# mLSTM mixer: turned rows one unit later, the gates' columns behind four tiles of values, the keys' last casts pinned

## The chip, the cores and the metric

The kernel runs on one core of a Trainium2 chip. The metric is the time of one execution in microseconds on the device, the median of several runs. TensorE (PE in the profile) does the matmuls and transposes, VectorE (DVE) and ScalarE (ACT) the elementwise work, GpSimd (POOL) some of it, and SyncE (SP) issues the transfers.

## What is computed

A network of two layers over 256 latent and 256 context tokens of width 1024: each layer is a half feed-forward, a mixer, and another half feed-forward, each with a residual norm. The first mixer is attention, the second the mLSTM that the change touches. Cut to that mixer:

```python
def mlstm_mixer(xl, xc, w_in, gate_b, conv_w, conv_b, norm_g, w_out):
    # p = xs @ w_in for both streams, split in q,k | v | o | g
    # q, k = silu(centred_conv(qk)); four heads, q and k of 128, v of 256
    # g: input and forget gates, forward and backward
    ...
    # forward and backward scans over the context, then over the latents
    o_lat = readout(hl_f + flip(hl_b), ol)

def readout(h, o):
    mu = jnp.mean(h, axis=-1, keepdims=True)
    var = jnp.mean(jnp.square(h - mu), axis=-1, keepdims=True)
    hn = (h - mu) * lax.rsqrt(var + LN_EPS)
    hn = hn.transpose(...).reshape(B, L, D_MODEL) * norm_g
    return (hn * jax.nn.sigmoid(o)) @ w_out
```

Per head and direction the scan is a masked, weighted product: with gate sums as exponents, `s = (q k^T) * exp(...)`, `num = s v`, `h = num / max(|sum of s|, exp(-m))`.

## The kernel before

**Tiling.** Activations stand transposed in `self.h`, eight tiles of 128 features by 512 tokens (latents in columns 0 to 255, context behind). Every float32 operand of a matmul is split into a high part (a cast to fp32r on ACT) and a low part (the rest, a subtraction on DVE), in `split` (lines 202 to 209). A product is then three matmuls, `mm3` (lines 221, 224, 225) or, with tokens as rows, `token_product` (lines 770 to 772): high by high, high by low, low by high. Weights are streamed in chunks of 128 by 1024: `raw` (line 189) loads one through SP's queue into one of three buffers, `chunk` splits it into one of seven buffers. `Keep` holds the chunks it has seen.

**What sets the order.** The program is written in the order of its data, and a scheduler of the framework lays out each engine's queue from it, by its own estimate of when operands are ready; each engine then runs its queue strictly in that order. `self.pin` ties an instruction behind the instruction that was written just before it on the same engine, and nothing else. So an instruction written later can still be queued earlier, unless it is pinned to one that is not.

**The mixer** (`mlstm`, from line 995). In order: queries, gates and keys are projected (`product`), latents first, while the norm of the context (`self.steps`, `norm`) is still being finished on ACT (line 496) and DVE (lines 495, 497); then the context half of the gates and keys. `gate_rows` (lines 1195 to 1235) turns the gates into rows of 64 by 512 on DVE and ACT; its `columns` (line 1237 on) transposes them (line 1240), and a copy (line 1242) leaves `kd` and `em`, the columns that later exponentials take as bias. Values follow: two blocks of four token tiles, 24 matmuls of 128 by 512 each; their casts are at line 1069, their low parts at line 1074. `residual` (lines 518 and 519) finishes the residual stream of an earlier norm, two tiles at a time.

**Units.** Eight units follow, head by head and in both directions: `inner` makes a head's scores (line 1082), the exponents in PSUM (lines 1092 and 1094), the weights by exponentials on ACT (lines 1099, 1112) and multiplications on DVE (lines 1102, 1114), their high parts (line 1104 on ACT, and `split`) and low parts (line 1105 on POOL, and `split`). `outer` of the unit before multiplies them by the values (lines 1127 to 1129), divides (lines 1131 to 1137), and, when both directions are summed, normalises the head's rows: statistics (1143, 1144), an inverse root of small DVE steps (233 to 247, 1146), and the scaling on ACT (line 1148). In the same step stand the products of the output gate (`OAT`, tanh at line 1171, line 1172 on POOL). `gated` transposes the head's normalised rows (line 1154, four transposes) and multiplies them by the gate on DVE (line 1157). Behind the units all eight tiles are split and multiplied by `w_out`: three output tiles first over inputs 0 to 5, then over inputs 6 and 7.

## Time and profile before

| | us |
|---|---|
| median of 3 runs | 1683.31 |
| lowest, highest | 1680.69, 1686.05 |
| the profiled execution | 1685.48 |
| its span, first to last instruction | 1683.7 |

The profiled execution's mean granted TensorE clock is 0.996. The mLSTM mixer takes about 1320 to 1483 us of the span. TensorE's busy time in parts of it (the windows of the trace):

| stretch, us | length | PE busy | granted clock |
|---|---|---|---|
| 1322 to 1364: queries, gates, keys, first values | 42 | 39.36 | 1.00 |
| 1364 to 1370: values, with the gates' columns | 6 | 6.00 | 1.00 |
| 1370 to 1400: values | 30 | 30.00 | 1.00 |
| 1400 to 1408: end of values, first unit | 8 | 7.50 | 1.00 |
| 1408 to 1470: units and the start of the out projection | 62 | 58.69 | 0.97 |

How to read it: a timeline row is start, duration, engine, line, operation and its tiles; in brackets stand the idle time of the engine ahead of it and what ended it. Matmuls overlap, so that the distance of their starts, not their duration, is the rate. A wait list row is who waited for whom, total, number, longest. A granted clock below 1.00 means that matmuls run slower by that factor.

### The profile page before, as it was taken

The numbers are of one execution on the slowest core, as the hardware profiler recorded it, in microseconds if no ns is written. First come the engines' busy times: TensorE is split into PE (matmuls) and PEld (weight loads), VectorE is DVE, ScalarE is ACT, GpSimd is POOL, SyncE is SP. The second block draws the span as 40 slices with busy tenths as digits, with TensorE's granted clock in tenths as the row PEclk, the third lists the DMA queues.
The fourth block names the chain that finished last, engine by engine and source line by source line (L and its number), as shares of the span: only waits on it lengthen the run. The fifth ranks groups of instructions, "written<-read, shape, count | busy, mean of one in ns | idle before, by whom it ended". The sixth has DMA issues, their size and how long they took to land.

```text
span 1683.7 us, 24582 instructions
## 1 busy us (share of the span) xinstructions
PE 1647.9 (98%) x9492; PEld 1441.9 (86%) x9492; DVE 1209.9 (72%) x2458; ACT 668.5 (40%) x1116; POOL 72.8 (4%) x82
## 2 busy tenths in 40 slices
PE   9999999999989999999999999999999999999998
PEld 6888888899977998888888998888889978999987
DVE  5899977659798889995334877643335866898687
ACT  5532123215665352222221443222222655656542
POOL 0000000001010100000000100000000101120000
PEclk9999999999999999999999999999999999999999
DMA  9577755412103247674222357642221332337552
GB/s 365 190 230 232 250 200 190 149 63 90 43 1 118 96 138 236 230 242 142 100 90 74 101 178 246 214 150 100 95 93 65 103 128 76 113 126 240 178 183 88
DMA packets 71909, 250.36 MB, mean 149 GB/s; under 512 B 7920, under 2 KB 10736, under 8 KB 71792
## 3 DMA queue, kind: packets, MB, share of 16 engines
q1 hardware_dynamic: 71216, 248.00, 43.5%
q8 instruction: 74, 1.21, 0.3%
q10 hardware_dynamic: 576, 0.79, 0.1%
q14 instruction: 43, 0.35, 0.1%
HBM read 247.71 MB, written 1.05 MB: 148 GB/s over the span
## 4 chain that ended last, share of the span: by engine, by line
PE 83%; DVE 10%; ACT 3%; issue 2%; DMA 1%; DVEq 0%; ACTq 0%; SPq 0%
PE t L221 23%; PE t L224 23%; PE t L225 23%; PE t L1255 4%; PE t L698 4%; DVE t L209 3%; ACT t L204 1%; PE t L771 1%; PE t L772 1%; PE t L770 1%; PE t L402 1%; DVE t L497 1%; DVE t L495 1%; DVE t L422 0%; DMA t<-in_ffn_in 0%
## 5 line engine op out<-in xcount | busy, mean ns | idle before, releaser
L221 PE MATMUL t<-t,t 128*128 128x512 f32 (+2 forms) x2532 | 852.8, 339 | 8.4 <-ACT t L204 5.8
L224 PE MATMUL t<-t,t 128*128 128x512 f32 (+2 forms) x2532 | 856.3, 339 | 1.2 <-DVE t L497 0.3
L225 PE MATMUL t<-t,t 128*128 128x512 f32 (+2 forms) x2532 | 853.1, 338 | 1.2 <-DVE t L209 1.1
L209 DVE TENSOR_TENSOR t<-t,t 128x256 fp32r<-128x256 f32 (+3 forms) x669 | 463.0, 726 | 203.8 <-ACT t L204 202.7
L204 ACT CAST t<-t 128x1024 fp32r<-128x1024 f32 (+3 forms) x453 | 377.1, 857 | 561.9 <-PE t L225 302.8
L221 PEld LDWEIGHTS t<-t,t 128*128 128x128 f32 x2532 | 475.9, 189 | 62.9 <-ACT t L204 8.0
L224 PEld LDWEIGHTS t<-t,t 128*128 128x128 f32 x2532 | 477.6, 189 | 55.8 <-DVE t L209 1.2
L225 PEld LDWEIGHTS t<-t,t 128*128 128x128 f32 x2532 | 477.2, 189 | 54.5 <-DVE t L209 2.1
L312 DVE SCALAR_TENSOR_TENSOR t<-t,t 128x1024 bf16<-128x1024 f32 x224 | 262.6, 1220 | 14.6 <-DMA t<-in_ada_w 14.0
L544 DVE TENSOR_TENSOR t<-t,t 128x512 f32<-128x512 f32 (+1 forms) x93 | 54.0, 585 | 116.1 <-PE t L225 95.7
L543 ACT ACTIVATE t<-t 128x512 f32<-128x512 f32 (+1 forms) x93 | 47.5, 514 | 196.7 <-PE t L225 196.6
L771 PE MATMUL t<-t,t 128*128 128x256 f32 (+1 forms) x256 | 79.3, 310 | 1.4 <-DVE t L209 1.4
L579 DVE SCALAR_TENSOR_TENSOR t<-t,t,t 128x256 f32<-128x256 f32 x96 | 42.7, 478 | 52.0 <-PE t L225 52.0
L770 PE MATMUL t<-t,t 128*128 128x256 f32 (+1 forms) x256 | 79.4, 310 | 0.0
L772 PE MATMUL t<-t,t 128*128 128x256 f32 (+1 forms) x256 | 78.9, 309 | 0.0
L439 POOL TENSOR_TENSOR t<-t,t 128x256 f32<-128x256 f32 x30 | 24.3, 809 | 1159.2 <-ACT t L429 1157.8
L1255 PE MATMUL t<-t,t 128*128 128x512 f32 (+3 forms) x286 | 60.8, 368 | 1.7 <-ACT t L1332 1.0
L698 PE MATMUL t<-t,t 128*128 128x512 f32 (+1 forms) x300 | 60.5, 364 | 0.0
L1255 PEld LDWEIGHTS t<-t,t 128*128 128x128 f32 (+2 forms) x286 | 43.8, 159 | 18.9 <-issue 3.6
L698 PEld LDWEIGHTS t<-t,t 128*128 128x128 f32 x300 | 51.5, 189 | 8.9
L429 ACT ACTIVATE t<-t 128x256 f32<-128x256 f32 x72 | 26.2, 412 | 66.9 <-DVE t L422 66.9
L771 PEld LDWEIGHTS t<-t,t 128*128 128x128 f32 x256 | 48.2, 188 | 4.4 <-DVE t L209 1.8
(191 smaller groups left out, 1082.7 us busy)
## 6 DMA issues: line engine op xcount, KB each, us to landing
t<-in_ffn_in SPq DMA_DIRECT2D x168, 512.0 KB, 4.1
t<-in_ada_w SPq DMA_DIRECT2D x137, 512.0 KB, 4.2
t<-in_ffn_out SPq DMA_DIRECT2D x66, 512.0 KB, 3.5
t<-in_ffn_last SPq DMA_DIRECT2D x22, 512.0 KB, 3.5
t<-in_att_in SPq DMA_DIRECT2D x12, 512.0 KB, 3.5
t<-in_att_out SPq DMA_DIRECT2D x8, 512.0 KB, 3.6
t<-in_ml_qk SPq DMA_DIRECT2D x8, 512.0 KB, 3.4
t<-in_ml_v SPq DMA_DIRECT2D x8, 512.0 KB, 3.5
```

The costliest lines, as they stand in the source:

```text
L204: self.behind(self.nc.scalar.copy(h, x))
L209: self.behind(self.nc.vector.tensor_tensor(out=ls, in0=xs, in1=hs.bitcast(F32), op=ALU.subtract))
L221: ins = mm(out, wh, xh, start=first, stop=False)
L224: mm(out, wh, xl, start=False, stop=False)
L225: mm(out, wl, xh, start=False, stop=last)
L312: ins = nc.vector.scalar_tensor_tensor(self.tmp().bitcast(BF16), r, 1.0, self.cb[:, v, :], ALU.mult, ALU.mult, accum_out=to)
L544: V.tensor_tensor(out=sl, in0=sl, in1=pu[:, :n], op=ALU.mult)
L698: pin(nc.tensor.matmul(o, gs[g], ws[k][w][:, i : i + n], start=k == k0 and g == w == 0, stop=k == k1 - 1 and g == 1,))
L770: mm(o, self.xh[:, k, c], wh, start=k == 0, stop=False)
L771: mm(o, self.xh[:, k, c], wl, start=False, stop=False)
L772: mm(o, self.xl[:, k, c], wh, start=False, stop=k == ND - 1)
L1255: mm = lambda *k, **kw: pin(nc.tensor.matmul(*k, **kw))
```

## The change

Five edits, all in the mixer:

- `gated` of head `hd` stood in step 2 hd + 3 of the unit loop; it stands in step 2 hd + 4, behind that step's output-gate product, and its transposes are pinned. The last head's stands behind the loop, which has two steps fewer.
- `columns` is called behind the fourth tile of values, not the second, and the exponential of `em` is written in it.
- The residual steps stand in the second block of values alone.
- The last two key chunks are loaded and split by two calls behind the norm, with their casts pinned (`w.pin`).
- `chunk` and `split` take that pin.

```diff
@@ -91,7 +91,7 @@
 LEADSTEP = {(0, 6): 'v', (2, 6): 'rxxxxxxxx'}
 ATTSTEP = {2: 'vrxxxxxxxx'}
 
-GATECOLS = (0, 1)
+GATECOLS = (0, 3)
 MLSTEP = {2: 'v', 3: 'rxxxxxxxx'}
 MIXAT = 20
 MLLEAD = 7
@@ -139,12 +139,13 @@
 
     def __init__(self, b, chunks, sh=0, seen=None):
         super().__init__(b, chunks, sh)
+        self.pin = lambda ins: ins
         self.all = dict([seen.kept]) if seen else {}
 
     def __call__(self, i, w=P):
         c, o = divmod(i * P, 1024)
         if c not in self.all:
-            self.all[c] = self.b.chunk(self.chunks[c], self.sh(c))
+            self.all[c] = self.b.chunk(self.chunks[c], self.sh(c), self.pin)
         h, l = self.all[c]
         return h[:, o : o + w], l[:, o : o + w]
 
@@ -194,14 +195,14 @@
         w = self.t([P, 2 * 1024 + BLOCK], dt, tag="w", bufs=WB)
         return [w[:, i * 1024 + sh : i * 1024 + sh + n] for i in range(2)]
 
-    def chunk(self, src, sh=0):
+    def chunk(self, src, sh=0, pin=lambda ins: ins):
         r = self.raw(src)
         h, l = self.pair(sh=sh)
-        self.split(r, h, l)
+        self.split(r, h, l, pin)
         return h, l
 
-    def split(self, x, h, l):
-        self.behind(self.nc.scalar.copy(h, x))
+    def split(self, x, h, l, pin=lambda ins: ins):
+        self.behind(pin(self.nc.scalar.copy(h, x)))
         n = 1 if x.shape[-1] != 1024 else FINE if self.fine else FINE0
         for i in range(n):
             c = slice(i * 1024 // n, (i + 1) * 1024 // n)
@@ -1041,6 +1042,10 @@
                 outs.append(o)
             assert not self.running
             self.fine = False
+
+            w.pin = self.pin
+            for i in range(MLLEAD - MH - 1, MH):
+                w(i * ND)
             for n, (ws, i, to) in enumerate(jobs):
                 if n < MH:
                     continue
@@ -1062,7 +1067,7 @@
                     self.token_product(o, ws, 512, tt)
                     if (blk, n) == GATECOLS:
                         columns()
-                    elif (blk, n) > GATECOLS:
+                    if blk:
                         self.residual(2, self.pin)
                     h = vh[:, tt, 2 * blk : 2 * blk + 2, 0:TL]
                     o2 = o.rearrange("p (n f) -> p n f", n=2)
@@ -1151,7 +1156,7 @@
                 tp = self.ps()
                 for tt in range(2):
                     for vv in range(2):
-                        nc.tensor.transpose(tp[:, vv * TL + tt * P : vv * TL + (tt + 1) * P], hs[tt][:, vv * P : (vv + 1) * P], self.ident)
+                        self.pin(nc.tensor.transpose(tp[:, vv * TL + tt * P : vv * TL + (tt + 1) * P], hs[tt][:, vv * P : (vv + 1) * P], self.ident))
                 for vv in range(2):
                     d = 2 * hd + vv
                     V.scalar_tensor_tensor(
@@ -1160,7 +1165,7 @@
 
             units = [(hd, dr) for hd in range(MH) for dr in range(2)]
             pws, hss = {}, {hd: [None, None] for hd in range(MH)}
-            for n in range(len(units) + 3):
+            for n in range(len(units) + 1):
                 if n < len(units):
                     pws[n] = inner(*units[n])
                 if 1 <= n <= len(units):
@@ -1170,9 +1175,10 @@
                     o = product(w_o, i, LAT)
                     S.activation(sg[:, i, :], o[:, :TL], AF.Tanh, scale=0.5)
                     nc.gpsimd.tensor_scalar(sg[:, i, :], sg[:, i, :], 0.5, 0.5, ALU.mult, ALU.add)
-                if n >= 3 and n % 2:
-                    hd = (n - 3) // 2
-                    gated(hd, hss[hd])
+
+                if n >= 4 and n % 2 == 0:
+                    gated(n // 2 - 2, hss[n // 2 - 2])
+            gated(MH - 1, hss[MH - 1])
             for d in range(ND):
                 self.split(sg[:, d, :], self.xh[:, d, 0:TL], self.xl[:, d, 0:TL])
             g = gate()
@@ -1228,13 +1234,13 @@
         scan(cm[B][:, ::-1], kd[B, 0:TL][:, ::-1], m0[B], ALU.max)
         em = t([64, TL])
         V.tensor_tensor(out=em, in0=sm[:, 0:TL], in1=cm, op=ALU.add)
-        S.activation(em, em, AF.Exp, scale=-1.0)
 
         self.cm = t([P, TL], F32R)
         S.copy(self.cm[0:64], cm)
         V.tensor_tensor(out=self.cm[64:P], in0=cm, in1=self.cm[0:64].bitcast(F32), op=ALU.subtract)
 
         def columns():
+            S.activation(em, em, AF.Exp, scale=-1.0)
             tp = self.ps()
             for i, x in enumerate([kd[:, i * P : (i + 1) * P] for i in range(4)] + [em[:, i * P : (i + 1) * P] for i in range(2)]):
                 self.pin(nc.tensor.transpose(tp[:, i * 64 : (i + 1) * 64], x, self.ident[0:64, 0:64]))
```

The first place is TensorE in unit 4, where head 0's rows are turned. `L1154` are the transposes, `L1092` and `L1094` unit 4's exponents, `L1127` to `L1129` the products of unit 3. Lines from 1046 on stand 5 or 6 lower in the changed file: 1154 is 1159 there, 1092 and 1094 are 1097 and 1099, 1127 to 1129 are 1132 to 1134. Before:

```order
L1082 MATMUL t_12618<-t_11527,t_11528 128x256 x2
L1154 MATMUL t_12610<-t_69,t_12409 128x128 x2
L1092 MATMUL t_12623<-t_11895,t_11523 128x512
L1154 MATMUL t_12610<-t_69,t_12428 128x128 x2
L1094 MATMUL t_12623<-t_11521,t_11522 128x2x128
L1127 MATMUL t_12648<-t_11529,t_12557 128x258
L1128 MATMUL t_12648<-t_68,t_12557 128x256
L1129 MATMUL t_12648<-t_11529,t_12558 128x258
```

Changed:

```order
L1087 MATMUL t_12611<-t_11527,t_11528 128x256 x2
L1097 MATMUL t_12616<-t_11904,t_11523 128x512
L1099 MATMUL t_12616<-t_11521,t_11522 128x2x128
L1132 MATMUL t_12641<-t_11529,t_12557 128x258
L1133 MATMUL t_12641<-t_68,t_12557 128x256
L1134 MATMUL t_12641<-t_11529,t_12558 128x258
```

The transposes of head 0 (of tiles 12409 and 12428) have left this place; they stand 45 rows further on, behind the 24 matmuls of an output-gate product (the last of them ahead), with unit 5's exponents behind:

```order
L226 MATMUL t_12698<-t_67,t_12701 128x256
L1159 MATMUL t_12730<-t_69,t_12409 128x128 x2
L1159 MATMUL t_12730<-t_69,t_12428 128x128 x2
L1097 MATMUL t_12737<-t_11904,t_11523 128x512
L1099 MATMUL t_12737<-t_11521,t_11522 128x2x128
L1132 MATMUL t_12762<-t_11529,t_12623 128x258
```

On VectorE ahead of that place stands the end of head 0's norm with unit 3's multiplication (`L1102`, 1107 in the changed file), whose tile 12553 the cast to tile 12557 reads. Before:

```order
L246 SCALAR_TENSOR_TENSOR t_12504<-t_12504,t_12501 128x2
L209 TENSOR_TENSOR t_13206<-t_13204,t_13206 128x1024
L247 SCALAR_TENSOR_TENSOR t_12503<-t_12504,t_12503 128x2
L1102 SCALAR_TENSOR_TENSOR t_12553<-t_12431,t_12553 128x512
L1146 SCALAR_TENSOR_TENSOR t_12514<-t_12494,t_12503 128x2
L1114 SCALAR_TENSOR_TENSOR t_12561<-t_12430,t_12561 128x128
L1114 SCALAR_TENSOR_TENSOR t_12568<-t_12430,t_12568 128x256
```

Changed:

```order
L247 SCALAR_TENSOR_TENSOR t_12504<-t_12504,t_12501 128x2
L210 TENSOR_TENSOR t_13206<-t_13204,t_13206 128x1024
L248 SCALAR_TENSOR_TENSOR t_12503<-t_12504,t_12503 128x2
L1107 SCALAR_TENSOR_TENSOR t_12553<-t_12431,t_12553 128x512
L1151 SCALAR_TENSOR_TENSOR t_12514<-t_12494,t_12503 128x2
L1119 SCALAR_TENSOR_TENSOR t_12561<-t_12430,t_12561 128x128
L1119 SCALAR_TENSOR_TENSOR t_12568<-t_12430,t_12568 128x256
```

Here nothing has moved: the multiplication keeps its place behind the low part of a weight chunk (128 by 1024).

The second place is VectorE at the last head's norm. `L1157` (1162 in the changed file) are head 2's multiplications by the gate, `L209` (210) low parts. Before:

```order
L233 TENSOR_SCALAR t_13127<-t_13120 128x2
L209 TENSOR_TENSOR t_68<-t_66,t_67 128x256
L240 TENSOR_SCALAR t_13129<-t_13127 128x2
L209 TENSOR_TENSOR t_68<-t_66,t_67 128x256
L241 SCALAR_TENSOR_TENSOR t_13130<-t_13129 128x2
L242 TENSOR_TENSOR t_13130<-t_13130,t_13127 128x2
L209 TENSOR_TENSOR t_13396<-t_13394,t_13396 128x1024
L243 SCALAR_TENSOR_TENSOR t_13131<-t_13130 128x2
L244 SCALAR_TENSOR_TENSOR t_13129<-t_13131,t_13129 128x2
L245 TENSOR_TENSOR t_13130<-t_13129 128x2
L246 SCALAR_TENSOR_TENSOR t_13130<-t_13130,t_13127 128x2
L247 SCALAR_TENSOR_TENSOR t_13129<-t_13130,t_13129 128x2
```

Changed:

```order
L234 TENSOR_SCALAR t_13120<-t_13113 128x2
L210 TENSOR_TENSOR t_68<-t_66,t_67 128x256
L241 TENSOR_SCALAR t_13122<-t_13120 128x2
L1162 SCALAR_TENSOR_TENSOR t_66<-t_13169,t_70,t_66 128x256
L242 SCALAR_TENSOR_TENSOR t_13123<-t_13122 128x2
L1162 SCALAR_TENSOR_TENSOR t_66<-t_13169,t_70,t_66 128x256
L243 TENSOR_TENSOR t_13123<-t_13123,t_13120 128x2
L210 TENSOR_TENSOR t_68<-t_66,t_67 128x256
L244 SCALAR_TENSOR_TENSOR t_13124<-t_13123 128x2
L210 TENSOR_TENSOR t_13396<-t_13394,t_13396 128x1024
L245 SCALAR_TENSOR_TENSOR t_13122<-t_13124,t_13122 128x2
L210 TENSOR_TENSOR t_68<-t_66,t_67 128x256
```

Head 2's two multiplications now stand inside the last head's chain; before, they stood ahead of its first step.

The third place is ScalarE at the keys' last casts. `L204` (205 in the changed file) casts a weight chunk, `L496` (497) writes the norm's output, `L1025` and `L1029` (1026, 1030) belong to the convolution. Before:

```order
L204 CAST t_11807<-t_11805 128x1024
L1025 ACTIVATE t_11661<-t_11608,t_70 128x256
L204 CAST t_11959<-t_11957 128x1024
L1029 ACTIVATE t_11527<-t_11661 128x256
L496 ACTIVATE t_67<-t_11701,t_11354 128x256
L496 ACTIVATE t_67<-t_11705,t_11354 128x256
L496 ACTIVATE t_67<-t_11709,t_11354 128x256
L496 ACTIVATE t_67<-t_11713,t_11354 128x256
L204 CAST t_11994<-t_11992 128x1024
```

Changed:

```order
L205 CAST t_11807<-t_11805 128x1024
L1026 ACTIVATE t_11661<-t_11608,t_70 128x256
L205 CAST t_11839<-t_11837 128x1024
L1030 ACTIVATE t_11527<-t_11661 128x256
L497 ACTIVATE t_67<-t_11701,t_11354 128x256
L497 ACTIVATE t_67<-t_11705,t_11354 128x256
L497 ACTIVATE t_67<-t_11709,t_11354 128x256
L497 ACTIVATE t_67<-t_11713,t_11354 128x256
L205 CAST t_11844<-t_11842 128x1024
```

The casts of the last two key chunks (tiles 11959 and 11994 before, 11839 and 11844 now) stand in the same places as before, the first of them ahead of the norm's output.

## The prediction

> **What bounds the kernel now.** I read the page's first and fourth parts, then the list of who waited for whom on TensorE in the stage that the diff touches, then short windows and the timeline there.
>
> ```profile
> span 1683.7 us, 24582 instructions
> PE 1647.9 (98%) x9492; PEld 1441.9 (86%) x9492; DVE 1209.9 (72%) x2458; ACT 668.5 (40%) x1116; POOL 72.8 (4%) x82
> PE 83%; DVE 10%; ACT 3%; issue 2%; DMA 1%; DVEq 0%; ACTq 0%; SPq 0%
> ```
>
> TensorE is busy 98% of the span and 83% of the chain that ended last is its own. The number of matmuls is not changed, so an edit can only win what TensorE now idles or runs slowly, or add to it. From 1310 to 1520 us (the mLSTM mixer with its neighbours) these are all its waits of note; the columns are the total, the number and the longest:
>
> ```profile
> PE t L1154 <- ACT t L1148: 3.0, 2, 2.3
> PE t L771 <- DVE t L209: 1.4, 1, 1.4
> PE t L225 <- DVE t L209: 1.1, 1, 1.1
> PE t L402 <- DVE t L379: 1.0, 2, 0.7
> PE t L1092 <- ACT t L1112: 0.5, 1, 0.5
> ...
> PE t L1129 <- POOL t L1105: 0.2, 1, 0.2
> ```
>
> That is 7.2 us. The first is the largest: the transposes of the normalised rows (L1154). Its clock price is seen in three windows (columns: stretch, length, busy time of PE, PEld, DVE, ACT, POOL, then PEclk, DMA share, GB/s):
>
> ```profile
> 1426.00:1429.00 3.00, 3.00 (x17) 2.96 (x17) 2.54 (x7) 2.87 (x9) 0.34 (x1) 0.60 0.12 49
> 1429.00:1432.00 3.00, 3.00 (x24) 3.00 (x23) 1.85 (x9) 0.81 (x3) 1.28 (x1) 0.83 0.00 0
> ...
> 1359.00:1363.00 4.00, 2.58 (x11) 1.80 (x10) 4.00 (x6) 3.26 (x6) 0.00 (x0) 1.00 0.06 12
> ```
>
> After the 2.28 us wait the granted clock is 0.60 and 0.83; after the 1.42 us wait near 1361 it stays 1.00.
>
> ```profile
> 1421.38 1.89 PE L1082 MATMUL t<-t,t 128*128 128x256 f32 x8
> 1425.55 0.44 PE L1154 MATMUL t<-t,t 128*128 128x128 f32 x2 [2.28 <-ACT t L1148]
> 1425.74 0.48 PE L1092 MATMUL t<-t,t 128*128 128x512 f32 x1
> 1426.06 0.42 PE L1154 MATMUL t<-t,t 128*128 128x128 f32 x2
> 1426.23 0.36 PE L1094 MATMUL t<-t,t 128*128 128x256 f32 x1
> 1426.43 0.28 PE L1127 MATMUL t<-t,t 128*128 128x258 f32 x1
> ...
> 1426.72 0.42 PE L1129 MATMUL t<-t,t 128*128 128x258 f32 x1
> ...
> 1429.94 0.32 PE L1129 MATMUL t<-t,t 128*128 128x258 f32 x1
> 1430.10 0.28 PE L1127 MATMUL t<-t,t 128*128 128x258 f32 x1
> 1430.21 0.28 PE L1128 MATMUL t<-t,t 128*128 128x256 f32 x1
> ...
> 1433.77 0.28 PE L1129 MATMUL t<-t,t 128*128 128x258 f32 x1
> ```
>
> From 1426.72 to 1429.94 lie 15 matmuls, 0.215 us each; right behind them the pitch is 0.11 to 0.12. The slow stretch costs 15 x 0.1 = 1.5 us. So head 0's wait is worth at most 2.28 + 1.5 = 3.8 us.
>
> The Trainium skill, "TensorE: Matmul & The Clock Gate" (section "What's actually happening"), says that the array's clock falls to half after an idle window of about 3.4 us and comes back after a busy one. The half rate agrees with the 0.215 us; a gap of 2.28 us was enough here, shorter than the 3.4 us that its section on HAM oscillation allows. By that allowance there would have been no clock loss and 2.28 us would be all that there is to win.
>
> **The change part by part.**
>
> *Rows turned one unit later.* In unit 4 the four L1154 transposes leave the place ahead of the products of unit 3 (L1127 to L1129). What comes next on TensorE are L1092 and L1094, then the first L1127, which reads the high part that L1104 casts, and the third, L1129, which reads the low part from L1105. When were those ready?
>
> ```profile
> 1423.65 0.68 DVE L1102 SCALAR_TENSOR_TENSOR t<-t,t 128x512 f32<-128x512 f32 x1
> ...
> 1424.37 0.62 ACT L1104 CAST t<-t 128x512 fp32r<-128x512 f32 x1 [2.96 <-DVE t L1102]
> 1424.89 1.09 ACT L1148 ACTIVATE t<-t,t,t 128x256 f32<-128x256 f32 x2
> ...
> 1425.07 1.27 POOL L1105 TENSOR_TENSOR t<-t,t 128x512 fp32r<-128x512 f32 x1 [5.46 <-ACT t L1104]
> ```
>
> The cast ends at 1424.99, barely ahead of the normalised rows, and the subtraction on POOL at 1426.34. All three hang on L1102 at 1423.65, which stands on DVE behind the norm's chain of head 0. The order on DVE up to there is the same in the changed kernel, so none of these times moves. TensorE then ends L1082 at 1423.27, does L1092 and L1094 (0.32 + 0.20 by their starts) to about 1423.8, waits 1.2 us for the cast, does two matmuls, and waits about 1.1 us for POOL. L1129 starts at 1426.40 in place of 1426.72: 0.32 us won. But the idle time is 2.3 us as before, so I take the clock loss as unchanged too. And the transposes have lost their cover: they ran inside the time in which POOL was still subtracting, and now run by themselves behind the unit's product of the output gate, at the price of a row where they had no wait:
>
> ```profile
> 1454.85 0.60 PE L1154 MATMUL t<-t,t 128*128 128x128 f32 x4
> 1455.20 0.36 PE L1127 MATMUL t<-t,t 128*128 128x258 f32 x1
> ```
>
> 0.35 us. Head 0 nets -0.32 + 0.35 = +0.03 us. Bounds: -3.8 (the wait and its clock go), +0.4 (transposes uncovered, nothing won).
>
> Heads 1 and 2 had no wait; their transposes cost the same 0.35 us a unit later: zero. On DVE their multiplications (L1157) now stand inside the next head's norm chain. What is queued behind such rows is L1102 of the next unit, and behind that cast, POOL and TensorE. The worst place is unit 4, whose L1102 now waits for unit 3's first tile of products: that tile ends about 1428.8 (nine matmuls of 0.215 us behind 1426.7), three small DVE rows of about 0.9 us follow, then 0.68 for L1102, 0.62 for the cast, 1.28 for POOL: 1432.3, against the 1433.77 at which TensorE's third product of unit 4 stood. The cover is 1.5 us; zero.
>
> *The last head.* Here the transposes end a chain that TensorE waits for.
>
> ```profile
> 1464.90 0.28 PE L224 MATMUL t<-t,t 128*128 128x256 f32 x1
> 1465.85 0.44 PE L1154 MATMUL t<-t,t 128*128 128x128 f32 x2 [0.67 <-ACT t L1148]
> ...
> 1455.33 1.04 ACT L204 CAST t<-t 128x1024 fp32r<-128x1024 f32 x1
> 1465.19 1.09 ACT L1148 ACTIVATE t<-t,t,t 128x256 f32<-128x256 f32 x2 [3.13 <-DVE t L1146]
> ...
> 1456.10 0.87 DVE L1157 SCALAR_TENSOR_TENSOR t<-t,t,t 128x256 f32<-128x256 f32 x2
> ...
> 1458.02 0.22 DVE L1131 SCALAR_TENSOR_TENSOR t<-t,t 128x1 f32<-128x1 f32 x1
> ...
> 1465.00 0.16 DVE L1146 SCALAR_TENSOR_TENSOR t<-t,t 128x2 f32<-128x2 f32 x1
> ```
>
> Head 2's two L1157 (0.87 us) ran ahead of the chain L1131 to L1146 and now stand in its middle. DVE's work up to L1146 is the same, so it ends no later than before but for idle time: without the pair, L209 waits for its cast, which ends at 1456.37, 0.27 us after the 1456.10 at which DVE would reach it. So L1146 ends 0.27 us later. On the other side, three more matmuls of the out projection stand ahead of the last transposes, 3 x 0.115 = 0.34 us. Net -0.07. New small waits for the low parts of inputs 4 and 5, which now come behind L1157 of head 2, fall inside the wait for the last transposes: laying the DVE rows one behind the other in the new order I get about 0.6 and 0.2 us. Bounds: -0.34 (no idle on DVE) and +0.87 (the whole pair on the path); I take -0.1, nearer the first since the pair only changes place.
>
> *Gate columns behind four tiles.* Six transposes and a copy move two tiles later. On TensorE they were back to back with the products; DVE's copy waited, with nothing urgent behind it:
>
> ```profile
> DVE t L1242 <- PE t L1240: 1.7, 1, 1.7
> ```
>
> Their first readers, unit 0's exponentials, need the scores, which stand behind all eight tiles. The exponential of em keeps its place on ACT and with it the table loads. The eight residual steps all fall into the second block, where TensorE has no wait in the list above. Zero; if the cover were gone, the transposes' 0.5 us.
>
> *The keys' last casts.* The intended target is visible:
>
> ```profile
> 1330.48 1.05 ACT L204 CAST t<-t 128x1024 fp32r<-128x1024 f32 x1 [3.59 <-DMA t<-in_ml_qk]
> ...
> 1331.75 1.70 ACT L496 ACTIVATE t<-t,t 128x256 fp32r<-128x256 f32 x4
> ...
> 1337.11 0.39 PE L225 MATMUL t<-t,t 128*128 128x256 f32 x1 [1.13 <-DVE t L209]
> ```
>
> A cast waits 3.59 us for its transfer, the norm's outputs (L496) stand behind it, and TensorE pays 1.13 us later. But the pin ties an instruction only to the last one written before it on its engine, here the cast of the key chunk before, which already stood ahead. The order on ACT is unchanged, so is SP's. Zero; bounds -1.13 and 0. The 1.42 us at L771 hangs on DVE rows that keep their order: it stays.
>
> **Sum.** +0.03 - 0.1 + 0 + 0 = about -0.1 us against the profiled execution: a span of 1683.6 us and 1685.4 us in place of 1685.48. The median of the runs is 1683.31 (1680.69 to 1686.05), which lies near the span; I forecast 1683.2 us. Differences under 0.3% (5 us) count as no change, since the runs of one kernel already spread that far.
>
> **Rivals.**
>
> *A: the wait goes.* If L1104 and L1105 come earlier than the rows say (DVE reaching L1102 sooner, once nothing waits for the transposes), the 2.28 us and the 1.5 us of slow clock go: 1683.3 - 3.8 = 1679.5 us. For it: it is the largest wait, and the turned rows were its releaser. Against: L1102 on DVE is not behind the transposes, and L1105's own 1.27 us ends after them.
>
> *B: the casts do move behind the norm's output.* L496 would not stand behind the transfer, and the 1.13 us vanish: 1682.2 us; with A, 1678.4. Against: the order on ACT.
>
> *C: slower, at the read-out's end.* If the low parts of inputs 4 and 5 and the last norm chain come later than laid out, TensorE's wait there grows from 0.67 by the pair's 0.87 and some 0.6 for the low parts to above 2 us within a few us. The point from which it decides lies between the 1.42 us of idle that left the clock at 1.00 and the 2.28 us that did not; past it comes another 1.5 us. Together 0.87 + 0.6 + 1.5 = +3.0: 1686.3 us. Against: DVE does the same work before L1146.
>
> **How the numbers follow.** Forecast 0.65, A 0.16, B 0.06, C 0.13. The range goes from A's 1679.5 to C's 1686.5; the forecast's own is 1681 to 1685. A and B lie mostly inside 0.3%; the part of them beyond 1678.3 (both together, or more clock than priced) gets 0.10, the part of C beyond 1688.4 gets 0.08, no change 0.82.
>
> **What would show it.** In the changed profile: no wait at head 0's transposes, but one of about 1.2 us of L1132 for ACT's cast (L1109) and one of about 1 us of L1134 for POOL (L1110), with the clock again near 0.6 for some 3.4 us. The last transposes wait for L1153 again, under 1 us. L226 still waits 1.1 us near 1337 behind a cast that waits for in_ml_qk, and L772 1.4 us near 1361. I am wrong if unit 4 shows neither the wait nor the slow clock, or if the read-out's end idles over 1.5 us.

## The result and the profile after

The changed kernel takes 1688.62 us (median of 8 runs, 1685.57 to 1691.43); the kernel before, run beside it, 1683.86 us. The ratio is 1.0029, 95% interval 1.0017 to 1.0041: slower, where -0.1 us was forecast. A second comparison with more runs (e5 below) gives 1.0018 (1.0009 to 1.0026), about 3 us. Both lie under the 0.3% that the prediction counts as no change, but both are clear of the noise, and 1688.62 us lies above the end of its range, 1686.5 us.

The profiled execution seems to show no loss. Span, busy times and the shares of the chain that ended last, from the page:

```profile
span 1683.8 us, 24582 instructions
PE 1645.8 (98%) x9492; PEld 1439.5 (85%) x9492; DVE 1209.9 (72%) x2458; ACT 668.2 (40%) x1116; POOL 73.2 (4%) x82
PE 81%; DVE 12%; ACT 3%; issue 2%; DMA 1%; POOL 0%; DVEq 0%; ACTq 0%; POOLq 0%
```

It was the fastest of the 8 runs, with a mean granted clock of 0.998 where the profile of before had 0.996. TensorE's share of the chain fell from 83 to 81%, DVE's rose from 10 to 12%. What TensorE waits for from 1310 to 1520 us (total, times, longest) tells more:

```profile
PE t L225 <- DVE t L210: 1.7, 2, 0.9
PE t L1132 <- ACT t L1109: 1.6, 2, 1.4
PE t L772 <- DVE t L210: 1.4, 1, 1.4
PE t L403 <- DVE t L380: 1.3, 2, 0.7
PE t L1134 <- POOL t L1110: 1.0, 2, 0.9
...
PE t L222 <- ACT t L205: 0.4, 1, 0.4
```

The first row was not there before. It stands at the start of the out projection. To compare the two executions without what the clock did in the first 1400 us, I set both to one mark, the matmul of unit 2's exponents that waits for ACT (L1092, 1097 in the changed file; the third of its eight). Rows of TensorE before:

```profile
1407.73 0.50 PE L1092 MATMUL t<-t,t 128*128 128x512 f32 x1 [0.50 <-ACT t L1112]
...
1457.68 0.29 PE L1129 MATMUL t<-t,t 128*128 128x258 f32 x1
...
1460.55 0.28 PE L221 MATMUL t<-t,t 128*128 128x256 f32 x1
1460.66 0.28 PE L224 MATMUL t<-t,t 128*128 128x256 f32 x1
...
1483.35 0.70 PE L402 MATMUL t<-t,t 128*128 128x256 f32 x2 [0.29 <-DVE t L379]
```

and in the changed kernel:

```profile
1403.91 0.50 PE L1097 MATMUL t<-t,t 128*128 128x512 f32 x1 [0.36 <-ACT t L1117]
...
1421.23 0.39 PE L1132 MATMUL t<-t,t 128*128 128x258 f32 x1 [1.43 <-ACT t L1109]
1422.59 0.58 PE L1134 MATMUL t<-t,t 128*128 128x258 f32 x1 [0.85 <-POOL t L1110]
...
1454.01 0.28 PE L1134 MATMUL t<-t,t 128*128 128x258 f32 x1
...
1457.23 0.36 PE L222 MATMUL t<-t,t 128*128 128x256 f32 x1
1458.45 0.39 PE L225 MATMUL t<-t,t 128*128 128x256 f32 x1 [0.85 <-DVE t L210]
...
1459.89 0.39 PE L225 MATMUL t<-t,t 128*128 128x256 f32 x1 [0.82 <-DVE t L210]
...
1461.60 0.50 PE L222 MATMUL t<-t,t 128*128 128x256 f32 x2 [0.40 <-ACT t L205]
...
1482.56 0.67 PE L403 MATMUL t<-t,t 128*128 128x256 f32 x2 [0.62 <-DVE t L380]
```

Behind the mark:

| place on TensorE | before | changed | difference |
|---|---|---|---|
| third product of unit 3 (L1129 / L1134) | 18.99 | 18.68 | -0.31 |
| last product of unit 7 | 49.95 | 50.10 | +0.15 |
| first matmul of the out projection (L221 / L222) | 52.82 | 53.32 | +0.50 |
| first matmul behind the out projection, of the next norm (L402 / L403) | 75.62 | 78.65 | +3.03 |

The first "before" number is 1426.72 (shown with the prediction) less 1407.73, and so on down. So the eight units cost next to nothing, and 2.5 us are lost inside the out projection, at a granted clock of 1.00 in both profiles. Its first matmul starts at 1457.23, its second, which reads the low part of the first input, 1.22 us later; before, the same two are 0.11 apart.

The low part comes late on DVE. Before (behind the rows that the prediction shows):

```profile
1450.69 0.15 DVE L1146 SCALAR_TENSOR_TENSOR t<-t,t 128x2 f32<-128x2 f32 x1
1450.76 0.68 DVE L1102 SCALAR_TENSOR_TENSOR t<-t,t 128x512 f32<-128x512 f32 x1
...
1454.96 1.23 DVE L209 TENSOR_TENSOR t<-t,t 128x1024 fp32r<-128x1024 f32 x1 [0.56 <-ACT t L204]
...
1456.89 1.22 DVE L209 TENSOR_TENSOR t<-t,t 128x1024 fp32r<-128x1024 f32 x1
...
1459.40 0.41 DVE L209 TENSOR_TENSOR t<-t,t 128x256 fp32r<-128x256 f32 x1
```

and in the changed kernel:

```profile
1446.36 0.48 DVE L1162 SCALAR_TENSOR_TENSOR t<-t,t,t 128x256 f32<-128x256 f32 x1
...
1446.83 0.48 DVE L1162 SCALAR_TENSOR_TENSOR t<-t,t,t 128x256 f32<-128x256 f32 x1
...
1448.50 0.69 DVE L1107 SCALAR_TENSOR_TENSOR t<-t,t 128x512 f32<-128x512 f32 x1
...
1451.34 0.15 DVE L1151 SCALAR_TENSOR_TENSOR t<-t,t 128x2 f32<-128x2 f32 x1
...
1454.58 2.56 DVE L210 TENSOR_TENSOR t<-t,t 128x1024 fp32r<-128x1024 f32 x2 [2.24 <-ACT t L205]
1457.07 0.21 DVE L1136 SCALAR_TENSOR_TENSOR t<-t,t 128x1 f32<-128x1 f32 x1
...
1457.99 0.41 DVE L210 TENSOR_TENSOR t<-t,t 128x256 fp32r<-128x256 f32 x1
```

The low part stands at 51.67 us behind the mark before and at 54.08 now. Before, its row ended at 1459.81 and it was read at 1460.66, 0.85 us of cover; now its row ends at 1458.40, 1.06 us after 1457.34, when TensorE would have read it (0.11 us behind its first matmul, as before). The reason is in the rows above it. Head 1's two multiplications (L1162) stand inside head 2's norm chain, whose last row (L1151) stands at 47.43 us behind the mark; before, that row (L1146) stood at 42.96. The pair itself is 0.87 us of these 4.5. Unit 7's scaled scores stand inside the chain too: L1107 runs at 1448.50, ahead of L1151, where L1102 came right behind L1146 before. ACT, before:

```profile
1450.88 1.09 ACT L1148 ACTIVATE t<-t,t,t 128x256 f32<-128x256 f32 x2 [1.46 <-DVE t L1146]
1451.88 0.60 ACT L1104 CAST t<-t 128x512 fp32r<-128x512 f32 x1
```

and in the changed kernel:

```profile
1449.22 0.62 ACT L1109 CAST t<-t 128x512 fp32r<-128x512 f32 x1 [3.96 <-DVE t L1107]
...
1451.53 1.09 ACT L1153 ACTIVATE t<-t,t,t 128x256 f32<-128x256 f32 x2 [1.18 <-DVE t L1151]
1452.52 0.82 ACT L1140 ACTIVATE t<-t,t 128x256 f32<-128x256 f32 x2
1453.24 0.38 ACT L1176 ACTIVATE t<-t 128x256 f32<-128x256 f32 x1
1453.50 1.05 ACT L205 CAST t<-t 128x1024 fp32r<-128x1024 f32 x1
```

The normalised rows of head 2 (L1153), unit 6's output (L1140) and the casts of two weight chunks stand in this order; the first cast starts 49.59 us behind the mark. DVE waits 2.24 us for it, splits two chunks (2.56 us), and only then reaches unit 7's rows and the low parts. In the profile before ACT did the normalised rows at 43.15 us, ahead of unit 7's cast.

### The profile page after: what moved, and what is told of

Its sections match the earlier page's. It is cut to its first block, busy times and chain, and to the rows that moved or that the text cites. A ratio compares the mean times of both kernels' runs of the same rounds, so it can differ in the third digit from the quotient of the medians.

```text
span 1683.8 us, 24582 instructions
## 1 busy us (share of the span) xinstructions
PE 1645.8 (98%) x9492; PEld 1439.5 (85%) x9492; DVE 1209.9 (72%) x2458; ACT 668.2 (40%) x1116; POOL 73.2 (4%) x82
## 3 DMA queue, kind: packets, MB, share of 16 engines
HBM read 247.71 MB, written 1.05 MB: 148 GB/s over the span
## 4 chain that ended last, share of the span: by engine, by line
PE 81%; DVE 12%; ACT 3%; issue 2%; DMA 1%; POOL 0%; DVEq 0%; ACTq 0%; POOLq 0%
PE t L225 22%; PE t L222 22%; PE t L226 22%; PE t L1261 4%; PE t L699 4%; DVE t L210 3%; ACT t L205 2%; PE t L772 1%; PE t L773 1%; PE t L771 1%; DVE t L496 1%; DVE t L498 1%; PE t L403 1%; DVE t L423 1%; DVE t L380 0%
## 5 line engine op out<-in xcount | busy, mean ns | idle before, releaser
L222 PE MATMUL t<-t,t 128*128 128x512 f32 (+2 forms) x2532 | 851.3, 339 | 8.5 <-ACT t L205 5.8
L226 PE MATMUL t<-t,t 128*128 128x512 f32 (+2 forms) x2532 | 851.9, 338 | 0.9 <-DVE t L210 0.8
L222 PEld LDWEIGHTS t<-t,t 128*128 128x128 f32 x2532 | 474.5, 188 | 63.7 <-ACT t L205 8.2
L226 PEld LDWEIGHTS t<-t,t 128*128 128x128 f32 x2532 | 475.6, 188 | 53.5 <-DVE t L210 1.5
L544 ACT ACTIVATE t<-t 128x512 f32<-128x512 f32 (+1 forms) x93 | 47.4, 514 | 194.8 <-PE t L226 194.8
L772 PE MATMUL t<-t,t 128*128 128x256 f32 (+1 forms) x256 | 79.0, 309 | 1.4 <-DVE t L210 1.4
L1261 PEld LDWEIGHTS t<-t,t 128*128 128x128 f32 (+2 forms) x286 | 43.7, 159 | 18.5 <-issue 2.7
L772 PEld LDWEIGHTS t<-t,t 128*128 128x128 f32 x256 | 48.2, 188 | 4.4 <-DVE t L210 1.8
```

Of the source, the lines that this page charges most:

```text
L222: ins = mm(out, wh, xh, start=first, stop=False)
L226: mm(out, wl, xh, start=False, stop=last)
L772: mm(o, self.xh[:, k, c], wl, start=False, stop=False)
L1261: mm = lambda *k, **kw: pin(nc.tensor.matmul(*k, **kw))
```

## The experiments

A ratio is to the kernel before, run beside it. "End" is the first L402 and "low part" the first one of the out projection's inputs, both in us behind the mark. "Slow from" is where the trace shows a stretch at half the granted clock in the mixer; it puts off what follows by about 1.1 us (the last product of unit 7 stands at 50.10 in the first changed profile and at 49.02 in e5, which has no such stretch ahead of it). So ends with and without one differ by that much for no other reason. The expectations call the mark "the start of unit 3"; by the count of L1092 rows it is unit 2's exponents, and the times are the same.

| run | ratio (95%) | low part | end | slow from |
|---|---|---|---|---|
| before, first profile | | 51.67 | 75.62 | 18.9 |
| changed, first profile | 1.0029 (1.0017 to 1.0041) | 54.08 | 78.65 | 18.2 |
| e1 turn alone | 1.0017 (1.0008 to 1.0025) | 54.06 | 78.65 | 18.2 |
| e2 gates' columns alone | 0.9994 (0.9983 to 1.0005) | 51.63 | 75.59 | 17.6 |
| e3 head 0 late | 1.0013 (1.0002 to 1.0025) | 52.66 | 76.75 | none |
| e4 heads 1, 2 late | 1.0001 (0.9991 to 1.0010) | 51.34 | 76.12 | 18.1 |
| e5 changed, again | 1.0018 (1.0009 to 1.0026) | 52.99 | 78.02 | 55.0 |
| e6 turn, pairs behind the chains | 1.0014 (1.0006 to 1.0023) | 53.12 | 77.92 | 19.5 |
| e7 turn, scores ahead of the norm | 1.0030 (1.0019 to 1.0041) | 53.87 | 78.73 | 55.3 |
| e8 heads 0, 1 late | 1.0018 (1.0008 to 1.0029) | 54.60 | 78.62 | 19.1 |
| e9 changed, two chunks tied | 1.0010 (1.0001 to 1.0019) | 51.12 | 76.11 | none |
| e10 before, two chunks tied | 0.9999 (0.9990 to 1.0009) | 51.51 | 75.80 | 18.5 |
| e11 before, five chunks tied | 0.9994 (0.9985 to 1.0003) | 50.41 | 74.78 | none |
| e12 before, 2.4 us added on DVE | 1.0018 (1.0009 to 1.0028) | 54.89 | 78.23 | 50.4 |
| e13 head 0 half a unit later, five tied | 0.9989 (0.9979 to 0.9998) | 50.02 | 74.30 | none |
| e14 the same, norm rows tied too | 0.9989 (0.9978 to 0.9999) | 50.62 | 74.91 | none |
| e15 = e11, again | 0.9989 (0.9977 to 1.0000) | 51.38 | 75.74 | 15.7 |

**Which part of the change.** e1 is the kernel before with the first edit only (gated, its transposes pinned, the loop two steps shorter); e2 with `GATECOLS`, the residual steps and the place of em's exponential only; e3 and e4 move some heads only:

```diff
-                if n >= 3 and n % 2:
-                    hd = (n - 3) // 2
-                    gated(hd, hss[hd])
+                for hd in range(MH):
+                    if n == (4, 5, 7, 9)[hd]:       # e3;  e4: (3, 6, 8, 9),  e8: (4, 6, 7, 9)
+                        gated(hd, hss[hd])
```

> The kernel before with only the turning of the rows one unit later (all four heads). Theory T1: turning heads 1 and 2 later puts their two multiplications into the next head's norm chain on DVE, the normalised rows of head 2 and the casts of the out projection's weights come some 3 to 4 us later, and the first low parts of the out projection's inputs with them; this is the whole loss: 1687 to 1689 us, 4 to 5 us above before, waits of L224 on L209 near 1458 us of about 0.8 us, two of them. Theory T2: the loss is in the gates' columns, the residual steps or the keys' casts: within 1.5 us of before. Theory T3: the loss is at head 0, whose transposes lost their cover while the wait and the slow clock stayed: as T1 in the time, but without new waits at the out projection.

> The kernel before with only the gates' columns behind four tiles of values (and the residual steps all in the second block). T1 and T3: within 1 us of before, 1683 to 1685 us. T2: 2 to 5 us above before.

> The kernel before with head 0 alone turned one unit later; heads 1, 2 and 3 as before. T1: within 1 us of before (+0.03 by the prediction's own sum), PE waits of 1.2 us for the cast and 1 us for POOL at unit 4, and the end of the read-out as before with one wait of about 0.7 us at the last transposes. T3: 2 to 5 us above before. T2: within 1 us.

> The kernel before with heads 1 and 2 alone turned one unit later; head 0 keeps its place and its wait of 2.3 us. T1: 3 to 5 us above before, with two waits of about 0.8 us of L224 on L209 at the start of the out projection. T2 and T3: within 1 us of before.

e1 has the changed kernel's low part and end to 0.02 us, and its ratio (1.0017, against 1.0018 in e5); e2 has the low part and the end of before, to 0.04 us. TensorE comes to the out projection 0.23 us sooner in e1 than in the changed kernel (53.09 and 53.32 us), waits 0.22 us longer for the first low part (1.07 and 0.85), and ends at the same time. The loss is the turn, which rules out T2. The keys' casts were not run alone; between e1 and the changed kernel, which has them, nothing at the mixer's end differs.

T1 in its first form falls with e4: heads 1 and 2 late cost nothing measurable, with no wait for low parts. Head 0 alone costs something, with a new wait at head 1's transposes, one unit on:

```profile
1437.40 0.44 PE L1154 MATMUL t<-t,t 128*128 128x128 f32 x2 [2.00 <-ACT t L1148]
```

Head 0's two multiplications are in head 1's norm chain there, whose last row (L1146) starts at 31.16 in place of 29.15 us; in e1 and the changed kernel at 32.2. With head 1 late as well this wait is not paid there but handed on: head 2's chain ends at 46.9 us (e8) or 47.4 (e1, changed), in place of 42.96. In e4, where head 0's pair is at its old place, it ends at 43.88. The delays add up only if they start at head 0. By its size e3 (2.2 us, interval 0.3 to 4.2) is nearer to T3's 2 to 5 us than to T1's under 1, but not for T3's reason: the clock stays at 1.00 in its whole stage, so that its end of 76.75 is about 2.2 us late at equal clock, and the wait that costs is the new one at head 1.

**How much is the pair.** e8 and e6, with e5 and e7 beside them. In e6 heads 0 and 1's multiplications are tied on DVE behind the end of the next head's chain, in e7 the norm is written behind the next unit's weights:

```diff
+                    self.after(V.scalar_tensor_tensor(                       # e6, in gated, heads 0 and 1
+                        sg[:, d, :], tp[:, vv * TL : (vv + 1) * TL], self.vec[:, V_NORMG + d : V_NORMG + d + 1], sg[:, d, :], ALU.mult, ALU.mult
+                    ), self.scale if hd < MH - 2 else None)                  # scale: L1146 of the last norm written
...
+                if n >= 3 and n % 2:                                         # e7, in the loop, behind inner
+                    norm(hss[(n - 3) // 2])
...
+                    self.after(V.bn_aggr(mv[:, tt, :], bs), self.prod if tt else None)   # prod: L1102
```

> The changed kernel once more, beside the kernel before on the same chip. If the loss is the rearranged tail of the mLSTM stage (3.0 us at the end of the out projection in its first profile and in the turn alone), the ratio is about 1.0018 (3 us), not the 1.0029 of the first comparison. If other parts of the change cost besides the turn, it is 1.0025 or more.

> The turn alone, with the two multiplications of heads 0 and 1 tied behind the end of the next head's norm chain on DVE (nothing else moves but those rows and ACT's normalised rows of head 2). Theory T1, as the first four runs left it: each pair inside the next head's chain makes that chain late, head after head, until the first low parts of the out projection are late. Then the chains of heads 1 and 2 end within 1.5 us of where the kernel before has them (29.2 and 43.0 us behind the start of unit 3), the two waits of 1.07 and 0.83 us at the out projection fall below 0.5 us together, and of the 3 us about 1.5 to 2.5 come back: ratio 1.0003 to 1.0009. Rival T4: the pair's place doesn't matter, the delay comes from the stall of PE at unit 4 and the weight chunks in between: the waits stay and the ratio is 1.0017 as for the turn alone.

> The turn alone, with each head's norm written behind the next unit's weights and the second half of its statistics tied behind that unit's scaled scores (L1102), so that the scores of unit 3 no longer stand behind the norm chain of head 0 on DVE. The prediction's reading (head 0's wait hangs on L1102 behind the chain, not on the transposes): the cast and POOL end some 2 us earlier, the waits of 1.4 and 0.85 us at unit 4 and the slow clock behind them go, 2 to 3.5 us less than the turn alone: ratio 0.9995 to 1.0006. If the chain is only made later by it: waits at the out projection above 2 us and a ratio of 1.0017 or more.

> Heads 0 and 1 turned one unit later, heads 2 and 3 as before. T1: head 1's chain ends 2 to 3 us later (head 0's pair is in it), head 2's about 4 us later (head 1's pair is in it), so head 2's transposes, still at their old place, wait 1 to 3 us on the way into unit 7, in place of the waits at the out projection: ratio 1.0010 to 1.0020. T4: no wait at head 2's transposes, ratio under 1.0010.

e5: the ratio is what the tail shows (78.02 and 78.65 against 75.62 us, 2.4 and 3.0 us), so nothing else of the change needs to cost. The first comparison's 4.8 us is within its interval of that.

e6: the chains of heads 1 and 2 are back at 29.83 and 43.59 us as T1 has it, one wait falls from 1.07 to 0.20, but the other stays at 0.83, and only 0.7 of the 3 us come back (77.92). Both theories miss: the pair moved out of the chain still stands on DVE ahead of unit 7's rows. Head 1's 0.87 us were done at 32.6 us before and are done at 43.7 now, right ahead of unit 7's scaled scores.

e7 did what rival A wanted of head 0, and it bought nothing (L1135 is the third product of unit 3 there, L227 and L230 are the first and second matmul of a product):

```profile
1421.00 0.39 PE L1135 MATMUL t<-t,t 128*128 128x258 f32 x1 [0.67 <-POOL t L1111]
1425.44 0.39 PE L227 MATMUL t<-t,t 128*128 128x256 f32 x1 [1.90 <-ACT t L1141]
...
1458.56 0.39 PE L230 MATMUL t<-t,t 128*128 128x256 f32 x1 [1.78 <-DVE t L209]
1460.00 0.58 PE L230 MATMUL t<-t,t 128*128 128x256 f32 x1 [0.81 <-DVE t L209]
```

The stall of 1.44 + 0.85 us at unit 4 is down to 0.67. But the norms end later (19.06 in place of 16.53 us at head 0), TensorE waits 1.90 us for unit 2's outputs behind them, and the two waits at the out projection are as long as 2.6 us together. Its ratio is the highest of all, though its interval overlaps the turn alone's.

e8: the waits came at the out projection (1.12 and 0.17 us) and at the last transposes (0.68), not at head 2's transposes as I wrote; the time was right.

**What sets the end.** In all ten profiles so far the end follows the first low part by 24 to 25 us. That is no proof, since the two share what lies ahead of them (and before, e2, e3 and e4 do not wait for it at all). So e9 and e10 move the low part alone: the weight chunks 4 and 5 of the out projection, which are read after three of eight output tiles, are split on DVE behind the low parts of the first four inputs. e11 also ties chunks 0 to 2, one of which stood inside each of three norm chains. e12 does the reverse and puts work of no use ahead of unit 7's scores:

```diff
+            self.after(low, self.tie)                                        # in split, on DVE's row
...
+            w.tie = lambda c: self.low[3] if c in (4, 5) else None           # e9, e10
+            w.tie = lambda c: self.scale[c] if c < 3 else self.low[3] if c in (4, 5) else None    # e11
...
+                if (hd, dr) == (3, 1):                                       # e12, in inner
+                    x = self.tmp()
+                    for _ in range(4):
+                        last = self.after(V.tensor_tensor(out=x, in0=kT[:, 3, :], in1=kT[:, 2, :], op=ALU.subtract), self.scale[2])
```

> The changed kernel, with the low parts of two weight chunks of the out projection (4 and 5, first read only after three of the eight output tiles) tied on DVE behind the low parts of its first four inputs. Theory T5, from the first eight runs: what sets the end of the out projection is when DVE comes to the first low part of its inputs (51.7 us behind the start of unit 3 in the kernel before, 53.0 to 54.1 in the changed one; the end follows 24 to 25 us later in all ten profiles). Then the first low part comes 1.5 to 2.5 us earlier, the two waits of 0.85 and 0.82 us go, the out projection ends at 75.5 to 76.8 us in place of 78.0 to 78.7, and the ratio falls from 1.0018 to between 0.9998 and 1.0010. Rival T6: the loss lies in TensorE's order and the stall at unit 4, and DVE only follows: ratio 1.0015 or more.

> The same tie in the kernel before. T5: TensorE does not wait for the first low parts there, so only the last transposes' wait of 0.67 us can go: ratio 0.9993 to 1.0000. T6: within 0.0005 of 1.

> The kernel before, with that tie, and the low parts of the out projection's weight chunks 0, 1 and 2 (one of 1.14 us stands inside the norm chain of each of heads 0, 1 and 2) tied behind the end of that chain. Head 0's chain ends 1.1 us earlier, the wait of 2.28 us at its transposes falls to about 1.1, and the clock stays up behind it (1.43 us of idle cost nothing near 1361 us), 1.5 us more: with the 0.67 us 2.5 to 3.3 us faster than before, ratio 0.9980 to 0.9986. If the wait is then set by L1102 (unit 3's cast) in place of the chain: 0.9990 or more.

> The kernel before, with four subtractions of 128x512 added on DVE (2.4 us, their output is not used) ahead of the last unit's scaled scores, and nothing else changed in TensorE's order. T5: the first low part moves from 51.7 to about 54 us, two waits for low parts appear at the out projection, which ends at 77.5 to 78.7 us: +2 to +3 us, ratio 1.0012 to 1.0020, the loss of the change without the change. T6: DVE has room there (it is busy 6.3 of 7 us in that unit): under +1 us.

e9: the low part comes at 51.12, both waits for low parts are gone, and one for a cast is left. DVE's rows in e9, the divisor of unit 7's output (L1149, L1131 before) and the first low part (L214):

```profile
1453.36 0.22 DVE L1149 SCALAR_TENSOR_TENSOR t<-t,t 128x1 f32<-128x1 f32 x1 [0.92 <-PE t L1147]
...
1456.19 0.43 DVE L214 TENSOR_TENSOR t<-t,t 128x256 fp32r<-128x256 f32 x1 [0.45 <-ACT t L209]
```

and TensorE's wait for the cast of input 4 (L209 there), with that cast, which waits for head 2's multiplication by the gate (L1175):

```profile
1460.02 0.87 ACT L209 CAST t<-t 128x256 fp32r<-128x256 f32 x2 [1.53 <-DVE t L1175]
...
1460.47 0.50 PE L235 MATMUL t<-t,t 128*128 128x256 f32 x2 [1.20 <-ACT t L209]
```

At unit 7 DVE now waits for TensorE. The end is at 76.11, 1.9 us ahead of e5, but about 1 us of that is the slow stretch that e5 has in the out projection. The first changed profile is the fair comparison, since neither has one there: from its first matmul to the end the out projection takes 25.33 us in it, 23.86 in e9 and 22.81 before. So 1.5 of the 2.5 us come back with the low parts alone, while TensorE's units are unchanged (last product of unit 7 at 49.03 us, in e5 at 49.02). What is left, 1.05 us, is about the wait of 1.20 for input 4, which stands behind head 2's turned rows; the late low parts had hidden most of it (0.40 in the changed kernel). The ratio fell from 1.0018 to 1.0010, at the edge of what T5 allowed; its interval still holds T6's 1.0015, so that the verdict rests on the trace.

e10: nothing gained; the low part was not waited for there, and the last transposes' wait, which was to go, grew from 0.67 to 0.94 us. Its ratio suits both theories. e12: 2.4 us more on DVE in the last unit make the kernel 1.0018, as the change did. The sum was right and the place not: TensorE waits in unit 7 itself, for the cast and for POOL (its first and third product, L1139 and L1141 there), and not for a low part.

```profile
1459.05 0.39 PE L1139 MATMUL t<-t,t 128*128 128x258 f32 x1 [0.68 <-ACT t L1116]
1461.07 0.39 PE L1141 MATMUL t<-t,t 128*128 128x258 f32 x1 [1.52 <-POOL t L1117]
```

So DVE has no room in the last unit, though it is busy 72% of the whole span, and T6's reading of e12 falls. But e12 does not show T5's step, the low part: it shows that a delay of DVE's rows there becomes TensorE's, at whichever row is read first. That the low parts are the row in the changed kernel is shown by its own waits and by e9.

e11 missed its 0.9980 to 0.9986: head 0's chain ends 1.5 us earlier (15.00), but the transposes now come ahead of the scores of unit 4 on TensorE, and the wait is 2.04 us there.

**Is the stall at unit 4 worth anything.** e13 writes head 0's transposes behind unit 4's scores and ties chunks 0 to 2 behind the scaled scores of units 3, 5 and 7; e14 also ties head 0's normalised rows on ACT behind unit 3's cast.

```diff
+                if n == 4:                                                   # behind inner(4), not in step 3
+                    gated(0, hss[0])
...
+            w.tie = lambda c: self.last[c + 1, 1] if c < 3 else self.low[3] if c in (4, 5) else None   # last: L1114
```

> The kernel before with head 0's transposes written behind the scores of unit 4 (half a unit later, not a whole one), the low parts of the out projection's weight chunks 0 to 2 tied on DVE behind the scaled scores of units 3, 5 and 7, and those of chunks 4 and 5 behind the low parts of the first four inputs. T5 (DVE's chain sets the tail): L1102 of unit 3 comes at 15.1 in place of 15.9 us, the third product of unit 4 some 0.8 us earlier, the tail is not later: the out projection ends at 73.5 to 75.0 us, ratio 0.9984 to 0.9996. Rival: head 0's stall is worth nothing, since what TensorE wins there it waits for later: 75.0 us or more, ratio 0.9997 or more.

> As the kernel with head 0's transposes behind the scores of unit 4, with the normalised rows of head 0 on ACT tied behind the cast of unit 3's weights, so that neither chain waits for the other. T5: the cast ends at 16.3 and POOL at 17.6 us behind the start of unit 3, in place of 17.2 and 18.6; the wait at unit 4 is 1.3 us in place of 2.3, and where the clock stays up another 1.5 us: the out projection ends at 72.5 to 74.5 us, ratio 0.9978 to 0.9992. Rival: the same as for the kernel without the tie, 0.9997 or more.

> The kernel before with the six weight chunks' low parts tied (chunks 0 to 2 behind the norm chains, 4 and 5 behind the first low parts) once more, beside the two others: 0.9990 to 0.9998, as its end of the out projection (74.8 us) says.

e13 came as expected, 0.9989: 1.9 us faster than before by the ratio, though its interval ends at 0.9998. Its end is 1.3 us earlier, but of that about 1.1 is the slow stretch that the profile of before has and e13's has not. The stall is still 1.61 us in it, and e11's second run (e15, which ties five chunks and not six) has the same ratio with a stall of 2.06. e14 gained nothing over e13: its stall is 1.95 and its end, 74.91, lies behind the 72.5 to 74.5 expected. So these three are the fastest versions here, ahead of both kernels and not told apart; what they share are the tied chunks. No run took the stall away without making DVE's rows later, so its worth stays open: e7 shows that it can be worth nothing, none shows it to be worth the 3.8 us of the prediction.

## Why the prediction was wrong

*The change's effect on head 0* was right: waits of 1.43 and 0.85 us (forecast 1.2 and 1.1) in place of 2.28, L1134 at 0.31 us earlier (forecast 0.32), the clock at 0.52 behind it, and the transposes uncovered. To the start of the out projection the changed kernel is 0.50 us late: -0.31, about 0.45 for the uncovered transposes (forecast 0.35), and a pause of some 0.3 us in unit 6's products (1444.13 to 1444.46), whose cause stays open.

*The columns and the casts* at zero were right as far as the mixer's end shows (e2; e1 against the changed kernel). The wait at L772 stayed at 1.4 us; L226's was 0.8.

*The step that failed* is the pair "Heads 1 and 2 had no wait ... zero" and "*The last head* ... I take -0.1". The prediction saw that the multiplications stand inside the next head's norm chain, and then followed only one thing queued behind them, L1102 to the cast, POOL and TensorE, and found 1.5 us of cover. It did not follow the chain's own end: the normalised rows on ACT, what stands behind them in ACT's queue (unit 6's output, two weight chunks' casts), and DVE's wait for these with unit 7's rows and the low parts behind. The sentence "DVE's work up to L1146 is the same, so it ends no later than before but for idle time" is where it went: the idle time is the matter. DVE now waits 2.24 us for the cast, where it waited 0.56, and L1146 of the last head starts at 60.20 in place of 57.27 us. The order on ACT was not looked at there, and head 2's normalised rows had moved behind unit 7's cast. The two terms were put at -0.1 together; the out projection measured +2.5, of which e9 gives 1.5 to the low parts and leaves about 1.0 at input 4. The prediction's own sign of being wrong, over 1.5 us of idle at the read-out's end, is there: the three waits at the out projection are 0.85, 0.82 and 0.40 us.

*Rival C* had the place, the sign and nearly the size (+3.0), with another mechanism, so that its size is luck: the low parts of inputs 4 and 5, and a wait at the last transposes with its slow clock. That wait is gone from the changed kernel, and its first profile has no slow clock there. In the main it was the first low parts, by the program's order those of inputs 0 and 1, which were not in the account at all since before the first had 0.85 us of cover that no row of a wait list shows. Head 2's inputs have a part (0.40 us for the cast of input 4, 1.20 in e9). C's chance of 0.13 was too small for a step whose bounds were +0.87 alone.

*Rival A* priced the stall at unit 4 as time of the whole kernel. e7 moved it and the time came back as other waits.

*The base* was off too. 1683.31 was the median of three runs; the medians of 35, 30, 34 and 29 runs of the same kernel, in the four rounds of experiments, were 1685.87, 1684.95, 1684.71 and 1685.24. C's +3.0 on 1685 is 1688, near the measured 1688.6; on 1683.3 it lay at the edge of the range.

## What to carry to other kernels

A row that is put into another chain delays that chain's last consumer: follow the chain to its end on every engine that reads it, and not only the first thing queued behind the moved row. In a stage where two engines hand work to and fro, a wait of the busiest engine need not be worth its length, since it can be slack of the other's chain (e7); adding a known amount of work of no use to the suspected engine (e12) shows in one run whether there is room, though not which row hands the delay on. A wait list shows the covers that are used up, not those that are nearly so: ahead of a move, look at how early the operands behind the moved place are ready.

## What the runs showed of the hardware

The granted clock is 1.00 or 0.50 in the mixer of these traces, and each slow stretch there lasts 3.41 us: in the profile of before it runs from 1426.59 to 1430.00 (the window 1426.60 to 1430.00 reads 0.50, 1430.10 to 1432.00 reads 1.00). The slow clock behind a stall is not a fixed price. In the first profile of the changed kernel it followed the stall at unit 4, in the second (e5, the same program) it did not, and came at the out projection. Windows (length, busy times, then granted clock third from the end) behind unit 4's stall and in the out projection, first profile:

```profile
1422.60:1425.60 3.00, 3.00 (x14) 3.00 (x15) 0.90 (x4) 2.15 (x7) 0.00 (x0) 0.52 0.03 11
...
1462.00:1465.00 3.00, 3.00 (x26) 2.85 (x25) 2.17 (x9) 0.70 (x3) 0.00 (x0) 1.00 0.73 223
```

and e5:

```profile
1426.50:1429.50 3.00, 3.00 (x25) 3.00 (x26) 1.89 (x7) 2.11 (x7) 0.00 (x0) 1.00 0.02 7
1462.00:1465.00 3.00, 2.34 (x11) 2.34 (x12) 3.00 (x15) 0.81 (x2) 0.00 (x0) 0.63 0.44 164
```

In 3 us TensorE did 14 matmuls at the one clock and 25 at the other, behind stalls of the same length to 0.03 us. e11 and e15, one program too, had 2.04 and 2.06 us of stall, then clocks of 1.00 and 0.50:

```profile
1422.61:1424.61 2.00, 2.00 (x11) 1.78 (x12) 2.00 (x7) 1.84 (x6) 0.09 (x1) 1.00 0.26 47
```

```profile
1421.76:1423.76 2.00, 2.00 (x7) 1.71 (x8) 1.90 (x6) 1.84 (x6) 0.09 (x1) 0.50 0.22 41
```

The ends of these two are 1.0 us apart. So the prediction's 1.5 us for the clock is a price that is paid in some executions, and 1.0 to 1.1 us of it were seen further on. Nor did the point from which it decides lie between one wait of 1.42 and one of 2.28 us, as rival C had it: in e5 the stretch begins at the end of two waits of 0.84 and 0.82 us with three matmuls between. The Trainium skill, "TensorE: Matmul & The Clock Gate" (section "What's actually happening"), has the clock drop behind an idle window of about 3.4 us; here stalls of 2.0 to 2.3 us were enough in some executions of a program and not in others.

Between runs of one program the mean granted clock moved too: the changed kernel's eight runs go from 0.998 (1685.57 us) to 0.995 (1691.43 us), some 2 us for each 0.001. A profile with a high clock hides a loss of 3 us, and only marks inside the stage showed it.
